# Sample tokens in the MLP's third quarter, a new order for the first up products, and two earlier edits in one kernel

## The chip, the cores and the metric

The kernel runs on one core of a Trainium2 chip. The metric is device time in microseconds (us) of that core for one launch. PE is the matrix engine, DVE the vector engine, ACT the scalar engine, POOL the general engine, SP the engine whose queue starts most transfers. L94 is line 94 of the kernel before.

## The reference, cut to what matters

One layer of an encoder for 1024 prompt frames (one new stream) and 64 sample frames (one running stream with 512 cached frames), 1088 tokens together, D = 1024, in float32. Prompt and sample have their own conditioning vector, so gates, shifts and scales differ between the two.

```python
mod = silu(c) @ w_ada + b_ada                 # shift1, scale1, gate1, shift2, scale2, gate2
h = rms_norm(x, g_norm1) * (1 + scale1) + shift1
proj = h @ w_in                               # parts for attention (MLA) and for gated linear attention (GLA)
a_out = attention(...)                        # low-rank q; latent keys and values; RMS norm of q and k per head
b_out = gla(...)                              # log_a = log_sigmoid(gate_lr @ w_gate_up + b_gate_up) / 16
x = x + gate1 * (concat(a_out, b_out) @ w_out)
h2 = rms_norm(x, g_norm2) * (1 + scale2) + shift2
x = x + gate2 * (square(relu(h2 @ w_up)) @ w_down)
```

Besides x, the new latents, rotary keys and the GLA states are returned.

## The kernel before, in words

**Products.** A float32 product is made of three products in a rounded format: each operand is split into a high part (a cast on ACT, helper line L102 or the line that calls it) and a low part (a subtraction on DVE, L103 or L106). L94, L95 and L96 are the three matmuls. PE's queue is the longest of all.

**Order of the program.** The kernel is written as generators (streams). `interleave` runs them in turns; each `yield pe, wait, cond` says how long PE is taken to work on what was just written, how long the stream then stands back, and what it waits for. A scheduling layer then sets each engine's order by its own costs, so an edit in one place also shifts instructions elsewhere. At run time every engine takes its queue strictly in order.

**Stages.** The first 85 us load x and weights and make q and k of GLA (the stream `shifts` loads the 1024-column rows of w_ada, 'raw', which L177 multiplies). Up to about 260 us GLA runs beside the other projections. It needs the gate weights 'wg' (zeroed on POOL at L615, then filled by a transfer in ACT's queue at L616 and one in SP's at L617), a pair of 'glrT' tiles (POOL, L620 and L621) and 'indi'. All of them stand in the pool 'big', whose room is free only when the first stage's tiles are done; L657 is the first product with wg.

**Keys.** `keys_values` (L960 on) makes keys and values of a tile of 128 tokens: four tiles of cached frames and the sample tile (`past_keys`, about 260 to 330 us), then eight prompt tiles beside attention (355 to 562 us). Two product groups g = 0, 1 give two heads each; ACT sums squares into 'ssk' (L984), POOL makes the reciprocal root of all four heads (L988, L989), DVE multiplies 'kn' (L991) and the rotary part 'krt' (L992) by it, and after `yield 0, 4500` PE transposes them (L998, L1005).

**Out projection and second norm.** Tokens are taken in four chunks of 272 (HW), in the order WORDER = (0, 2, 1, 3); half h = c // 2. Chunks 1 and 3 end in 32 sample tokens each, so their parts list has two entries, and each operation with a conditioning vector is done twice. `main` loads GLA's and attention's outputs ('mx') and the output gate ('mr') of the next chunk, makes its operands 'mh' and 'ml', multiplies by w_out, adds into x (L1456), stores it and adds squares into 'acc' (ACT L1463, DVE L1464). `norm2` makes of that sum a row scale (L1478 to L1489) and then h2 (DVE L1495, ACT L1497). Its last chunk, 3, runs beside the first products of the up projection.

**MLP.** Both projections use seven products of half matrices in place of eight (Strassen's scheme). Up: token operands 'ah' and 'al' number 0 to 6 (`tokens`), weights per block j of 128 columns (`weights`, `put`), products (`up`). The order is written by hand: blocks 0 and 1 do products 0 to 3 for the first half of the columns, then for the second, then 5, 4, 6 block by block; blocks 2 to 15 do 0, 1, 2, 5, 3, 4, 6. The results go to memory ('u_d') and are read back for down, whose sums are scaled and added at L1910 and stored at L1914.

## Time and profile before

| | us |
|---|---|
| three runs, median (lowest to highest) | 1357.65 (1357.14 to 1358.04) |
| the profiled execution's own time | 1358.17 |
| its span | 1356.4 |
| PE busy in the span | 1325.8 (98%) |
| DVE, ACT, POOL busy | 894.9, 655.3, 64.5 |
| granted clock of PE over the span | 0.996 |

The profiled execution's time is 1.8 us over its span, and 0.5 us over the median of the runs. PE's busy time is the time in which at least one matmul is under way; what is left of the span, 30.6 us, is idle time of PE. In the timeline a row ends with the idle time ahead of it and with what ended that: `[1.58 <-DVE kn L991]`. A row with x4 merges four instructions. The granted clock (PEclk) says which share of full speed PE was allowed.

### The profile page before, as it was taken

The page shows a single profiled execution, that of the slowest core. Times are in us where ns is not written, and L with a number is a line of the kernel's source. Part 1 is how long each engine was busy: PE and PEld are TensorE (multiplying, and loading weights), DVE is VectorE, ACT ScalarE, POOL GpSimd, SP SyncE. Part 2 cuts the span into 40 slices and gives each one's busy share as a digit, 9 for nine tenths or more (in the row PEclk, how much of TensorE's full clock was granted, in tenths as well). Part 3 has the DMA queues.
Part 4 walks back from the last instruction along what each step waited for, and adds up shares of the span by engine and source line. Part 5 has one row for each costly group of instructions (what it writes and reads, how often), then busy time and mean ns, then how long its engine had stood idle before and what let it go on. Part 6 is the DMA issues. An engine that isn't in the chain of part 4 may idle for free.

```text
span 1356.4 us, 25887 instructions
## 1 busy us (share of the span) xinstructions
PE 1325.8 (98%) x10052; PEld 1257.9 (93%) x10052; DVE 894.9 (66%) x1926; ACT 655.3 (48%) x1634; POOL 64.5 (5%) x110
## 2 busy tenths in 40 slices
PE   9999999989999999999989999999999999999998
PEld 8899999878867788999989999999999999999998
DVE  4898787465576656677799565665636865874554
ACT  5465545443255656753575445444443333433432
POOL 0110010121111100000000000000000000000000
PEclk9999999999999999999999999999999999999999
DMA  9420123324445320573417443444349845543441
GB/s 343 137 74 1 48 76 90 107 83 126 153 129 171 96 89 16 163 209 111 137 40 232 141 156 128 160 139 138 115 168 341 282 152 192 162 125 92 132 124 34
DMA packets 155110, 183.64 MB, mean 135 GB/s; under 512 B 16063, under 2 KB 106475, under 8 KB 154987
## 3 DMA queue, kind: packets, MB, share of 16 engines
q1 hardware_dynamic: 147530, 176.44, 41.0%
q10 hardware_dynamic: 7456, 5.54, 1.3%
q8 instruction: 79, 1.29, 0.4%
q14 instruction: 45, 0.36, 0.1%
HBM read 130.71 MB, written 51.23 MB: 134 GB/s over the span
## 4 chain that ended last, share of the span: by engine, by line
PE 82%; DVE 7%; DMA 4%; ACT 4%; POOL 2%; issue 1%; SPq 0%; ACTq 0%; DVEq 0%; POOLq 0%
PE mm L94 14%; PE mm L96 13%; PE mm L95 13%; PE g L94 6%; PE g L96 6%; PE g L95 6%; PE tp L94 3%; PE tp L95 3%; PE tp L96 3%; PE mm L1076 3%; PE g L1103 2%; PE mm L177 1%; PE g L881 1%; PE tp L1113 1%; POOL ssk L989 1%
## 5 line engine op out<-in xcount | busy, mean ns | idle before, releaser
L102 ACT CAST opers<-quad 128x512 fp32r<-128x512 f32 x112 | 69.4, 620 | 184.6 <-PE mm L96 145.1
L103 DVE TENSOR_TENSOR opers<-quad,opers 128x512 fp32r<-128x512 f32 x112 | 77.2, 690 | 112.3 <-ACT opers L102 112.3
L96 PE MATMUL mm<-opers 128*128 128x272 f32 x448 | 128.9, 288 | 0.0
L94 PE MATMUL mm<-opers 128*128 128x272 f32 x448 | 128.6, 287 | 0.3 <-DVE e L1910 0.3
L95 PE MATMUL mm<-opers 128*128 128x272 f32 x448 | 128.3, 286 | 0.0
L94 PE MATMUL mm<-ah,wh 128*128 128x272 f32 x424 | 122.5, 290 | 2.0 <-ACT wh L102 1.7
L95 PE MATMUL mm<-al,wh 128*128 128x272 f32 x424 | 121.8, 288 | 0.3 <-DVE al L103 0.3
L96 PE MATMUL mm<-ah,wl 128*128 128x272 f32 x424 | 121.6, 288 | 0.0
L94 PE MATMUL mm<-hh,wh 128*128 128x384 f32 (+2 forms) x264 | 90.6, 344 | 0.7 <-ACT wh L321 0.7
L95 PE MATMUL mm<-hl,wh 128*128 128x384 f32 (+2 forms) x264 | 87.2, 330 | 0.0
L96 PE MATMUL mm<-hh,wl 128*128 128x384 f32 (+2 forms) x264 | 86.9, 330 | 0.0
L94 PEld LDWEIGHTS mm<-opers 128*128 128x128 f32 x448 | 84.6, 189 | 0.5 <-issue 0.5
L96 PEld LDWEIGHTS mm<-opers 128*128 128x128 f32 x448 | 84.3, 188 | 0.0
L95 PEld LDWEIGHTS mm<-opers 128*128 128x128 f32 x448 | 84.1, 188 | 0.0
L94 PEld LDWEIGHTS mm<-ah,wh 128*128 128x128 f32 x424 | 80.0, 189 | 3.1 <-ACT wh L102 2.2
L95 PEld LDWEIGHTS mm<-al,wh 128*128 128x128 f32 x424 | 79.8, 188 | 0.5 <-DVE al L103 0.5
L96 PEld LDWEIGHTS mm<-ah,wl 128*128 128x128 f32 x424 | 79.8, 189 | 0.0
L103 DVE TENSOR_TENSOR opers<-ru,opers 128x544 fp32r<-128x544 f32 x108 | 77.6, 719 | 2.2 <-ACT opers L102 2.0
L102 ACT CAST opers<-ru 128x544 fp32r<-128x544 f32 x108 | 69.4, 643 | 13.1 <-PE mm L96 11.7
L102 ACT CAST wh<-ru 128x512 fp32r<-128x512 f32 x67 | 41.1, 618 | 65.7 <-PE g L95 24.6
L103 DVE TENSOR_TENSOR wl<-ru,wh 128x512 fp32r<-128x512 f32 x67 | 45.9, 689 | 35.5 <-ACT wh L102 35.3
L94 PE MATMUL mm<-wh,hh 128*128 128x264 f32 (+3 forms) x216 | 65.9, 305 | 0.0
(410 smaller groups left out, 4241.5 us busy)
## 6 DMA issues: line engine op xcount, KB each, us to landing
ru<-u_d SPq DMA_DIRECT2D x108, 272.0 KB, 2.9
raw<-in_w_ada SPq DMA_DIRECT2D x40, 512.0 KB, 4.2
ru<-in_w_up SPq DMA_DIRECT2D x32, 512.0 KB, 4.1
quad<-in_w_down SPq DMA_DIRECT2D x16, 1024.0 KB, 7.2
u_d<-st SPq DMA_DIRECT2D x60, 272.0 KB, 2.1
u_d<-sc SPq DMA_DIRECT2D x45, 272.0 KB, 2.2
raw<-in_w_in SPq DMA_DIRECT2D x22, 256.0 KB, 3.8
x<-in_xo_T SPq DMA_DIRECT2D x8, 544.0 KB, 6.1
```

The source lines that it names most:

```text
L94: pin(PE.matmul(out, lhsT=ah, rhs=bh, start=first, stop=False, skip_group_check=more))
L95: pin(PE.matmul(out, lhsT=ah, rhs=bl, start=False, stop=False, skip_group_check=more))
L96: pin(PE.matmul(out, lhsT=al, rhs=bh, start=False, stop=last, skip_group_check=more))
L102: ACT.copy(hi, src)
L103: eng.tensor_tensor(out=lo, in0=src, in1=f32(hi), op=ALU.subtract)
L177: mm = PE.matmul(acc[32 * j:32 * j + 32, 0:256], lhsT=scT[:, k, :], rhs=was[k][:, 256 * j:256 * (j + 1)], start=(k == 0), stop=(k == KT - ...
L881: PE.matmul(sc[:n, a, p], lhsT=d[:, w * p + n * a:w * p + n * a + n], rhs=qv[:, :, p, a], start=True, stop=True)
L989: POOL.tensor_tensor(out=ss[:n, 4:8], in0=ss[:n, 4:8], in1=mhalf[:n], op=ALU.pow)
L1076: PE.matmul(sp[:n, :w], lhsT=x[:, hd, :n], rhs=y[:, hd, :w], start=(j == 0), stop=(j == 4))
L1103: PE.matmul(op[:n, 0:P], lhsT=pt[:kw, k, :n], rhs=kvs[kt // 4].v[:kw, kt % 4, hd], start=(kt == 0), stop=(kt == nkt - 1))
L1113: PE.transpose(tp[:kw, k, :n], pr[k0 // 4][:n, P * k:P * k + kw], ident[:n, :n])
```

## The change

Four edits:

1. GLA's constants wg, glrT and indi move to the pool 'gqkp', which exists from the start. POOL zeroes wg and glrT at the start, and SP starts the three transfers right behind the third chunk of x.
2. In `keys_values` POOL makes the reciprocal root of each pair of heads as soon as the pair's squares are there, and DVE multiplies kn and krt pair by pair. The wait ahead of the transposes becomes a parameter, `ahead`: 7000 for the cached frames and the sample tile, 4500 as before for the prompt's tiles.
3. The 64 sample tokens all stand at the end of chunk 2 (the third quarter, second in WORDER); chunks 0, 1 and 3 hold prompt tokens alone. The waits ahead of the norm's first product grow from 2500 to 4500 in all chunks but the last. Down's sums follow: the first half of the tokens has one span, the second three pieces.
4. Blocks 0 and 1 do products 4, 5, 6 in that order, both blocks in each. `weights` and `tokens` follow that order ("w 4" comes before tokens 5, "w 5" before tokens 6). Block 1's products 5 and 6 go to the bank pair tp instead of g; pool st2 has three buffers.

```diff
+    wg = gqkp.tile([97, 256], F32, name="wg")
+    POOL.memset(wg, 0.0)
+    glrT = [gqkp.tile([97, 320], F32, name=f"glrT{j}") for j in range(2)]
...
+    indi = gqkp.tile([P, 2], F32, name="indi")
...
             load_x(2)
+            SP.dma_start(wg[0:16], I["w_gate_up"])
+            SP.dma_start(wg[96:97], I["b_gate_up"])
+            SP.dma_start(indi, I["gla_ind"])
...
-        wg = big.tile([97, 256], F32, name="wg")
-        POOL.memset(wg, 0.0)
-        ACT.dma_start(wg[0:16], I["w_gate_up"])
-        SP.dma_start(wg[96:97], I["b_gate_up"])
...
-    def keys_values(lh, ll, ki, tab, n, kv, slot):
+    def keys_values(lh, ll, ki, tab, n, kv, slot, ahead=4500):
...
+            POOL.tensor_scalar(out=ss[:n, 4 + 2 * g:6 + 2 * g], in0=ss[:n, 2 * g:2 * g + 2], scalar1=ss[:n, 8:9],
+                               scalar2=192 * EPS, op0=ALU.add, op1=ALU.add)
+            POOL.tensor_tensor(out=ss[:n, 4 + 2 * g:6 + 2 * g], in0=ss[:n, 4 + 2 * g:6 + 2 * g], in1=mhalf[:n, 0:2], op=ALU.pow)
             yield 1300, 0, None
-        POOL.tensor_scalar(out=ss[:n, 4:8], in0=ss[:n, 0:4], scalar1=ss[:n, 8:9], scalar2=192 * EPS, op0=ALU.add, op1=ALU.add)
-        POOL.tensor_tensor(out=ss[:n, 4:8], in0=ss[:n, 4:8], in1=mhalf[:n], op=ALU.pow)
...
+        for g in range(2):
+            DVE.tensor_tensor(out=kn[:n, 2 * g:2 * g + 2], in0=kn[:n, 2 * g:2 * g + 2], in1=rs[g], op=ALU.mult)
...
-        yield 0, 4500, None
+        yield 0, ahead, None
...
     def place(c):
-        h, hs = divmod(c, 2)
-        if hs == 0:
-            return h, HALVES[0], ((0, 512 * h, HW, 0),)
-        return h, HALVES[1], ((0, 512 * h + HW, 512 - HW, 0), (1, SEQ + 32 * h, 32, 512 - HW))
+        t0 = c * HW
+        parts = {2: ((0, t0, HW - DEC, 0), (1, SEQ, DEC, HW - DEC)), 3: ((0, t0 - DEC, HW, 0),)}
+        return c // 2, HALVES[c % 2], parts.get(c, ((0, t0, HW, 0),))
...
-                yield 0, 2500, None
+                yield 0, 2500 if end else 4500, None
...
             for j, x in ((4, 22), (5, 21), (6, 12)):
+                if j > 4:
+                    yield 0, 0, has(f"w {j - 1}")
...
-                if j < 2:
-                    yield from put(j, 5, b11, DVE)
                 sub(t2, b21, t2, DVE)
                 yield from put(j, 4, t2, DVE)
+                done.add(f"w 4 {j}")
                 yield 0, 1500, None
+                if j < 2:
+                    yield from put(j, 5, b11, DVE)
+                    done.add(f"w 5 {j}")
+                    yield 0, 1500, None
...
-                    side[j, h] = g_bank()[:, 0:HT // 2]
+                    side[j, h] = (tp_bank if j == 1 else g_bank)()[:, 0:HT // 2]
...
-            order += [(j, i, h) for j in range(2) for i in (5, 4, 6) for h in range(2)]
+            order += [(j, i, h) for i in (4, 5, 6) for j in range(2) for h in range(2)]
...
-        SPANS = ((0, 0, 512), (1, 512, HT))
+        SPANS = (((0, 0, HT),), ((0, 0, HW - DEC), (1, HW - DEC, HW), (0, HW, HT)))
```

What moves, at three places. PE at the first tile of cached frames, around the transposes of kn; before:

```order
L94 MATMUL mm<-wh,hh 128x320
L95 MATMUL mm<-wl,hh 128x320
L998 MATMUL tp<-ident,kn 128x128 x4
L96 MATMUL mm<-wh,hl 128x320
L1005 MATMUL tp<-ident,krt 128x128 x4
L94 MATMUL mm<-wh,hh 128x320
```

and of the change:

```order
L96 MATMUL mm<-wh,hl 128x320
L1001 MATMUL tp<-ident,kn 128x128 x2
L94 MATMUL mm<-wh,hh 128x320
L1001 MATMUL tp<-ident,kn 128x128 x2
L95 MATMUL mm<-wl,hh 128x320
L96 MATMUL mm<-wh,hl 128x320
L94 MATMUL mm<-wh,hh 128x320
L95 MATMUL mm<-wl,hh 128x320
L96 MATMUL mm<-wh,hl 128x320
L1008 MATMUL tp<-ident,krt 128x128 x4
```

The transposes stand in two pairs, and the rotary part's come five matmuls later. From the tile's last latent product (with a few transposes of a latent among them) to the first transposes of kn stand, over the four tiles of cached frames, 20, 18, 18 and 30 matmuls of the projections before, and 18, 31, 48 and 45 now.

DVE at the end of chunk 0's sum of squares in the out projection ('ml0' is the low part of the third chunk's operand, 'acc' the sum); before:

```order
L1456 SCALAR_TENSOR_TENSOR x12_6700<-mm_6848,modT_98,x12_6700 128x272
L1464 TENSOR_TENSOR acc_6735<-acc_6735,sq_6875 128x272
L103 TENSOR_TENSOR ml0_7174<-mx_6888,mh0_7173 128x1088
L1481 TENSOR_SCALAR st_6927<-tp_6923 128x2
L1481 TENSOR_SCALAR st_6927<-tp_6923 16x1
```

and of the change:

```order
L1457 SCALAR_TENSOR_TENSOR x12_6752<-mm_6903,modT_98,x12_6752 128x272
L103 TENSOR_TENSOR ml0_7234<-mx_6943,mh0_7233 128x1088
L1465 TENSOR_TENSOR acc_6790<-acc_6790,sq_6930 128x272
L1271 TENSOR_TENSOR mx_6944<-mx_6944,mr_6945 128x1088
L1457 SCALAR_TENSOR_TENSOR x21_6753<-mm_6950,modT_98,x21_6753 128x208
L1457 SCALAR_TENSOR_TENSOR x21_6753<-mm_6950,modT_98,x21_6753 128x64
L1482 TENSOR_SCALAR st_6996<-tp_6992 128x2
```

The third chunk's operand now stands ahead of the last addition to the sum, and on ACT its gate's silu stands ahead of the last two squares (before: of the last one). PE's product with the sum (L1478, now L1479) comes 12 matmuls later in its queue.

DVE at the start of the up projection, from the sums of half matrices to the token operands 5 ('al4' to 'al6' are their low parts, 'wl' slots hold weights, 'tw' is the half-made weight of product 4); before:

```order
L1392 TENSOR_TENSOR x21_6701<-x21_6701,x22_6702 128x4x272
L106 TENSOR_TENSOR x12_6700<-x12_6700,x22_6702 128x4x272
L103 TENSOR_TENSOR wl0_7833<-ru_7844,wh0_7832 128x512
L1394 TENSOR_TENSOR x12_6700<-x12_6700,x11_6699 128x4x272
L106 TENSOR_TENSOR tw_7934<-ru_7844,tw_7934 128x512
L103 TENSOR_TENSOR al4_8062<-x22_6702,ah4_7810 128x272 x8
L1686 TENSOR_TENSOR st_7900<-st_7900,g_8138 128x272
L103 TENSOR_TENSOR al5_8096<-x21_6701,ah5_7795 128x272 x8
L103 TENSOR_TENSOR wl1_7835<-tw_7934,wh1_7834 128x512
L103 TENSOR_TENSOR al6_8129<-x12_6700,ah6_7794 128x272 x8
```

and of the change:

```order
L1393 TENSOR_TENSOR x21_6753<-x21_6753,x22_6754 128x4x272
L106 TENSOR_TENSOR x12_6752<-x12_6752,x22_6754 128x4x272
L103 TENSOR_TENSOR wl0_7874<-tw_7975,wh0_7873 128x512
L1395 TENSOR_TENSOR x12_6752<-x12_6752,x11_6751 128x4x272
L1698 TENSOR_TENSOR st_7941<-st_7941,g_8141 128x272
L103 TENSOR_TENSOR al4_8087<-x22_6754,ah4_7851 128x272 x8
L106 TENSOR_TENSOR tw_8022<-ru_7924,tw_8022 128x512
L1698 TENSOR_TENSOR st_7983<-st_7983,g_8175 128x272
L103 TENSOR_TENSOR al5_8122<-x21_6753,ah5_7836 128x272
L103 TENSOR_TENSOR wl1_7876<-tw_8022,wh1_7875 128x512
L103 TENSOR_TENSOR al5_8122<-x21_6753,ah5_7836 128x272 x7
L103 TENSOR_TENSOR wl2_7878<-ru_7885,wh2_7877 128x512
```

Product 4's weight for block 0 now stands ready ahead of its tokens, block 1's comes behind them; before, block 0's came behind the tokens of product 5, and operand 6 ahead of any weight for it. On PE the products stand one behind the other, where before those of several products alternated: 130 matmuls lie between the last chunk's broadcast (L1489, now L1490) and the first of product 4.

More of the change, by code (lines that the diff above doesn't have):

```diff
@@ L252, in layer @@
     h, gqk = {}, []
+    wg = gqkp.tile([97, 256], F32, name="wg")
+    POOL.memset(wg, 0.0)
+    glrT = [gqkp.tile([97, 320], F32, name=f"glrT{j}") for j in range(2)]
+    for t in glrT:
+        POOL.memset(t[0:96], 0.0)
+        POOL.memset(t[96:97], 1.0)
+    indi = gqkp.tile([P, 2], F32, name="indi")
     def w_in_cols(a, b):
@@ L613, in layer @@
         bcum = big.tile([P, 2, TOK], F32, name="bcum")
-        wg = big.tile([97, 256], F32, name="wg")
-        POOL.memset(wg, 0.0)
-        ACT.dma_start(wg[0:16], I["w_gate_up"])
-        SP.dma_start(wg[96:97], I["b_gate_up"])
-        glrT = [big.tile([97, 320], F32, name=f"glrT{j}") for j in range(2)]
-        for t in glrT:
-            POOL.memset(t[0:96], 0.0)
-            POOL.memset(t[96:97], 1.0)
         masks = big.tile([P, 6, 64], I32, name="masks")
         ACT.dma_start(masks, I["gla_masks"][:, 1:7])
-        indi = big.tile([P, 2], F32, name="indi")
-        ACT.dma_start(indi, I["gla_ind"])
         SBk = [big.tile([P, 2, 256], F32, name=f"SB{i}") for i in range(3)]
@@ L985, in keys_values @@
             DVE.tensor_copy(kv.v[:n, slot, 2 * g:2 * g + 2], pg[:, :, P:2 * P])
+            POOL.tensor_scalar(out=ss[:n, 4 + 2 * g:6 + 2 * g], in0=ss[:n, 2 * g:2 * g + 2], scalar1=ss[:n, 8:9],
+                               scalar2=192 * EPS, op0=ALU.add, op1=ALU.add)
+            POOL.tensor_tensor(out=ss[:n, 4 + 2 * g:6 + 2 * g], in0=ss[:n, 4 + 2 * g:6 + 2 * g], in1=mhalf[:n, 0:2], op=ALU.pow)
             yield 1300, 0, None
-        POOL.tensor_scalar(out=ss[:n, 4:8], in0=ss[:n, 0:4], scalar1=ss[:n, 8:9], scalar2=192 * EPS, op0=ALU.add, op1=ALU.add)
-        POOL.tensor_tensor(out=ss[:n, 4:8], in0=ss[:n, 4:8], in1=mhalf[:n], op=ALU.pow)
-        rs = ss[:n, 4:8].rearrange("p (h o) -> p h o", o=1).broadcast_to([n, H, P])
-        DVE.tensor_tensor(out=kn[:n], in0=kn[:n], in1=rs, op=ALU.mult)
-        DVE.tensor_tensor(out=kr[:n], in0=R[:n].rearrange("p t d c -> p t (d c)").broadcast_to([n, H, P]),
-                           in1=rs, op=ALU.mult)
+        rs = [ss[:n, a:a + 2].rearrange("p (h o) -> p h o", o=1).broadcast_to([n, 2, P]) for a in (4, 6)]
+        for g in range(2):
+            DVE.tensor_tensor(out=kn[:n, 2 * g:2 * g + 2], in0=kn[:n, 2 * g:2 * g + 2], in1=rs[g], op=ALU.mult)
+        for g in range(2):
+            DVE.tensor_tensor(out=kr[:n, 2 * g:2 * g + 2], in0=R[:n].rearrange("p t d c -> p t (d c)").broadcast_to([n, 2, P]),
+                              in1=rs[g], op=ALU.mult)
         cs = slice(P * slot, P * slot + n)
-        yield 0, 4500, None
+        yield 0, ahead, None
         tp = heads(tp_bank())
@@ L1158, in past_keys @@
             yield 220, 1000, None
-            yield from keys_values(lh, ll, 8 + t, t, P, kvS[0], t)
+            yield from keys_values(lh, ll, 8 + t, t, P, kvS[0], t, 7000)
         yield from new_keys(8)
@@ L1169, in new_keys @@
         if i == 8:
-            yield from keys_values(lh, ll, 12, 4, n, kvN[0], 0)
+            yield from keys_values(lh, ll, 12, 4, n, kvN[0], 0, 7000)
         else:
@@ L1545, in layer @@
         wq = uctx.enter_context(tc.tile_pool(reuse_waits="tile", name="wq", bufs=1))
-        st2_ = pool("st2", 2)
+        st2_ = pool("st2", 3)
         warr = {}
@@ L1626, in rest @@
                 yield 0, 1500, None
+                sub(t2, b21, t2, DVE)
+                yield from put(j, 4, t2, DVE)
+                done.add(f"w 4 {j}")
+                yield 0, 1500, None
                 if j < 2:
                     yield from put(j, 5, b11, DVE)
-                sub(t2, b21, t2, DVE)
-                yield from put(j, 4, t2, DVE)
-                yield 0, 1500, None
+                    done.add(f"w 5 {j}")
+                    yield 0, 1500, None
                 yield from put(j, 6, b22, DVE)
@@ L1643, in weights @@
                     step = next(r)
+            for i in (4, 5):
+                yield 0, 0, has(f"tokens {i} 1")
+                for j, r in ((0, a), (1, b)):
+                    while f"w {i} {j}" not in done:
+                        yield next(r)
+                done.add(f"w {i}")
             yield 0, 0, has("tokens 6 1")
@@ L1717, in product @@
                         relu2("22", 6, True)
-                if i == 4 and h:
+                if i == (5 if j < 2 else 4) and h:
                     a11, a21, a22 = acc.pop((j, "11")), acc.pop((j, "21")), acc.pop((j, "22"))
@@ L1906, in out @@
             e = OUT[c][:, m]
-            for s, c0, c1 in SPANS:
+            for s, c0, c1 in SPANS[th]:
                 c0, c1 = max(c0, h * HW), min(c1, h * HW + HW)
@@ L1936, in _tables @@
     return {"k_rope_tab": np.ascontiguousarray(tab), "gla_masks": masks, "gla_ind": ind}
-ORDER = np.r_[0:512, SEQ:SEQ + 32, 512:SEQ, SEQ + 32:TOK]
+ORDER = np.r_[0:752, SEQ:TOK, 752:SEQ]
 _OUTS = [("y_T", (D, TOK), None),
```

1 line of the change is left out of this document (removed).

## The prediction

> **What bounds the kernel now.** I read first how busy each engine is in each stage (a table by stretches of the span; the first three columns are length, PE's busy time with its count of instructions, and weight loads, then DVE, ACT, POOL; the last three are granted clock, DMA share, GB/s).
>
> ```profile
> core 0: us, PE busy (x) PEld busy (x) DVE busy (x) ACT busy (x) POOL busy (x), PEclk, DMA share, GB/s
> 0.00:85.00 85.00, 81.56 (x643) 73.59 (x644) 60.45 (x146) 43.86 (x86) 4.79 (x12) 1.00 0.61 204
> 85.00:260.00 175.00, 170.83 (x1221) 160.76 (x1220) 131.54 (x305) 93.09 (x324) 16.86 (x30) 1.00 0.22 64
> 260.00:330.00 70.00, 63.81 (x393) 56.82 (x392) 42.92 (x107) 33.64 (x130) 14.28 (x26) 1.00 0.33 94
> 355.00:562.00 207.00, 199.19 (x1402) 160.62 (x1402) 139.80 (x406) 125.76 (x397) 23.58 (x34) 0.99 0.38 117
> 562.00:681.00 119.00, 117.19 (x918) 115.99 (x917) 82.19 (x180) 59.66 (x125) 4.75 (x8) 0.99 0.52 154
> 681.00:716.00 35.00, 31.52 (x221) 29.61 (x222) 33.28 (x80) 24.57 (x65) 0.24 (x1) 0.95 0.22 65
> 716.00:1353.00 637.00, 636.68 (x5098) 636.27 (x5096) 396.89 (x689) 271.60 (x507) 0.00 (x0) 1.00 0.49 158
> ```
>
> PE sets the time everywhere. The number of matmuls hardly changes (7 rows more of 8542 in PE's order), so a gain can only be PE's idle time, length minus busy: 3.4, 4.2, 6.2, 7.8, 1.8, 3.5 and 0.3 us in these stages. The last 637 us have nothing to give. A second loss hides inside busy time: where the granted clock is below 1, PE works slower. Two-microsecond stretches show it (columns: length, PE busy, clock, DMA share, GB/s):
>
> ```profile
> 596.00:598.00 2.00, 2.00 (x16) 0.88 1.09 372
> 598.00:600.00 2.00, 2.00 (x11) 0.50 1.11 279
> 600.00:602.00 2.00, 2.00 (x13) 0.77 0.63 208
> 404.00:406.00 2.00, 2.00 (x10) 0.50 0.50 129
> 704.00:706.00 2.00, 1.76 (x8) 0.50 0.36 139
> ```
>
> Around 598 the clock is halved for 0.48 + 2.00 + 0.92 = 3.4 us (twice the missing share of each row) and PE loses 2 x (0.12 + 0.50 + 0.23) = 1.7 us. The same happens around 404 and 704. The two of 598 and 704 come right behind waits which this change works on.
>
> **The change part by part: GLA's constants.** PE waits at the first gate product; the second row is the transfer's issue, the third its size and microseconds to landing:
>
> ```profile
> 91.51 1.10 PE L657 MATMUL g<-glrT,wg 97*128 97x256 f32 x4 [1.06 <-POOL SB L629]
> 87.97 0.43 ACTq L616 DMA_DIRECT2D wg<-in_w_gate_up  x1
> wg<-in_w_gate_up ACTq DMA_DIRECT2D x1, 16.0 KB, 3.4
> 43.32 0.64 PE L177 MATMUL mm<-raw,scT 128*32 128x256 f32 x8 [1.19 <-DMA raw<-in_w_ada]
> ```
>
> The first row names POOL, but 87.97 + 3.4 = 91.4 is when PE starts: it is the transfer. With the issue at the start of the kernel, 1.06 us go. In PE's new order 18 matmuls instead of 14 stand ahead of the fourth group of L177: four more, at 81.56 / 643 = 0.13, take 0.5 of its wait of 1.19. The three added issues stand in SP's queue ahead of the loads of w_ada; at 0.43 each they would cost 1.3 if SP had no time there, and this wait would grow by as much. The stage's DMA share of 0.61 leaves room, so I take no delay and keep 1.3 as the end. Together -1.6 (+0.2 to -2.3).
>
> **Keys.** Waits for the multiplied keys at L998 (total, times, longest; first those of 255 to 330 us, then those of 355 to 562 with another wait of that stage), and the chain ahead of the first:
>
> ```profile
> PE tp L998 <- DVE kn L991: 4.0, 3, 1.6
> ```
>
> ```profile
> PE tp L1113 <- ACT prob L1087: 3.5, 3, 1.2
> PE tp L998 <- DVE kn L991: 1.7, 2, 0.9
> ```
>
> ```profile
> 271.14 0.31 POOL L988 TENSOR_SCALAR ssk<-ssk 128x4 f32<-128x4 f32 x1 [3.70 <-ACT krt L984]
> 271.53 1.03 POOL L989 TENSOR_TENSOR ssk<-ssk,mhalf 128x4 f32<-128x4 f32 x1
> 272.60 0.69 DVE L991 TENSOR_TENSOR kn<-kn,ssk 128x512 f32<-128x512 f32 x1 [1.11 <-POOL ssk L989]
> 273.44 0.63 PE L998 MATMUL tp<-ident,kn 128*128 128x128 f32 x4 [1.58 <-DVE kn L991]
> 266.88 0.55 POOL L122 TENSOR_TENSOR s<-s,mhalf 128x1 f32<-128x1 f32 x1
> 268.01 0.42 DVE L700 TENSOR_TENSOR lat<-cn,gkv_bc 128x256 f32<-128x256 f32 x1
> ```
>
> From the last square to kn the work was 0.31 + 1.03 + 0.69 = 2.03. The power of one column took 0.55 and of four 1.03, so two are about 0.71 (0.55 + 0.48 / 3); half of kn is 0.42. The chain of the second pair becomes 0.31 + 0.71 + 0.42 = 1.44, 0.6 shorter. At the first tile two fewer matmuls stand ahead, at 63.81 / 393 = 0.16 that is 0.3 lost, but two transposes and a matmul (0.3 + 0.16) now cover the second pair: 1.58 - 0.6 + 0.3 - 0.45, about 0.8, is left. The next two tiles have 13 and 30 more matmuls ahead, 2.1 and 4.8 us, more than any of these waits. So 4.0 becomes 0.8: -3.2. For the prompt's tiles `ahead` is unchanged; the shorter chain takes 0.6 of each of two waits: -1.2 (0 to -1.7). DVE pays 2 x 0.42 - 0.69 = 0.15 twice on each of 13 tiles, 3.9 us, and POOL as often a second start; DVE's 139.80 busy of 207 and 42.92 of 70 hide it. If DVE were the late one there, all of this gain would turn round (rival A).
>
> **The sum of chunk 0 in the out projection.** PE waits 1.78 for it, and DVE had waited for ACT's last square:
>
> ```profile
> 595.75 0.71 PE L1478 MATMUL tp<-ones,acc 128*128 128x1 f32 x6 [1.78 <-DVE acc L1464]
> 595.16 0.44 DVE L1464 TENSOR_TENSOR acc<-acc,sq 128x272 f32<-128x272 f32 x1 [2.57 <-ACT sq L1463]
> 593.70 1.11 ACT L1267 ACTIVATE mr<-mr 128x1088 f32<-128x1088 f32 x1 [1.99 <-DMA mr<-r_d]
> 595.03 1.08 ACT L102 CAST mh<-mx 128x1088 fp32r<-128x1088 f32 x1
> 596.15 1.29 DVE L103 TENSOR_TENSOR ml<-mx,mh 128x1088 fp32r<-128x1088 f32 x1 [0.54 <-ACT mh L102]
> 588.34 1.20 SPq L1418 DMA_DIRECT2D mr<-r_d  x2
> 587.03 1.28 DVE L1268 TENSOR_TENSOR mx<-mx,mr 128x1088 f32<-128x1088 f32 x1
> ```
>
> The last square stood behind a silu that waited for a transfer, whose buffer came free when L1268 ended (587.03 + 1.28, the issue at 588.34). Two things now pull against each other. PE's product comes 12 matmuls later, 12 x 117.19 / 918 = 1.5 us. But cast and subtraction of the next operand stand ahead of the last square's addition: with the silu still at 593.70 the sum would be done at about 593.70 + 1.11 + 0.4 + 1.08 + 1.29 + 0.44 = 598.0, 2.4 later than before (595.16 + 0.44), and the wait would grow by 0.9. In DVE's new order, however, the gate's multiplication stands ahead of a subtraction (1.29) and an addition, so the transfer starts some 1.7 earlier and so does the silu: the sum comes 0.7 later, PE 1.5 later, and 1.0 of the wait goes (bounds +0.9 and -1.78). A remaining 0.8 is below the waits followed by a half clock; I take that stretch of 1.7 us as gone.
>
> The chunk with the samples now comes second, with three SP issues and twice the DVE additions more. The stage's idle time of 1.8 is the 1.78 of this one wait, so no other operand was late. I put that at nothing; uncovered it is the three issues, at most 3 x 0.6 = 1.8.
>
> **The start of up.** DVE prepares the last chunk and the operands, PE waits at the products:
>
> ```profile
> 681.47 0.93 PE L1489 MATMUL tp<-last,ones 128*128 128x128 f32 x6
> 682.43 3.13 DVE L1495 SCALAR_TENSOR_TENSOR x<-x,G,tp 128x240 f32<-128x240 f32 x11
> 687.48 1.31 DVE L1495 SCALAR_TENSOR_TENSOR x<-x,G,tp 128x32 f32<-128x32 f32 x5
> 698.20 0.68 DVE L106 TENSOR_TENSOR tw<-ru,tw 128x512 f32<-128x512 f32 x1
> 698.80 2.90 DVE L103 TENSOR_TENSOR al<-x,ah 128x272 fp32r<-128x272 f32 x8
> 700.27 0.39 PE L94 MATMUL mm<-ah,wh 128*128 128x272 f32 x1 [1.30 <-ACT wh L102]
> 702.11 0.39 PE L94 MATMUL g<-ah,wh 128*128 128x272 f32 x1 [1.01 <-DVE st L1686]
> ```
>
> Before, the low half of operand 4 began to come at 698.80 + 0.36 (2.90 / 8) = 699.2. Now 8 operations of 272 columns replace 16 (4.44 together; 8 x 0.4 = 3.2, so -1.2), the half-made weight (-0.68) moves behind, one addition of a result, 0.4, comes ahead: 697.7 by the old clock. PE has 130 x 0.128 = 16.6 us of matmuls after 681.47 + 0.93 and reaches product 4 at 699.0. The operand is there, by a margin of 1.3. Block 1's weight follows at 697.7 + 2.5 + 0.68 and a cast, about 701.5; PE needs it after 48 matmuls, at 705.1. Of the stage's 3.5 us of idle time I leave 0.4, less than one operation, for some late operand: -3.1. With the waits the half clock at 704 goes: -1.7.
>
> [...]
>
> **Sum.** -1.6 - 3.2 - 1.2 - 1.0 - 1.7 - 3.1 - 1.7 = -13.5. Against it: in three stages (85 to 260, 260 to 330, 355 to 562) the scheduling layer has shifted many instructions, and waits like those of L1113 for ACT's 'prob' in attention (3.5 in three, above) can arise or go. I allow one such wait, 3.5 / 3 = 1.2, per stage: +3.5 (0 to +7). Net -10.0. The profiled execution took 1358.17 (span 1356.4 and 1.8 around it), 0.5 over the median, so 1348.2 by the profile and **1347.7** as a median.
>
> **The rivals.** 0.2% is 2.7 us, about what a measurement of this kernel tells from no change; the bounds are 1354.9 and 1360.4.
>
> A: in the first 560 us waits only change place. DVE and ACT carry the same chains, and a later transpose lets the next group's operand be late. For it: attention has 7.8 of idle time spread over several causes; against it, DVE is at 68% there. Then the first two parts' 6.0 are lost, with no allowance beside it: -7.5, 1350.2.
>
> B: the half clock stays. For it: the wait of 1.58 at 273.44 lies in a stage whose clock reads 1.00, so a wait alone doesn't decide. Against it: all three stretches follow waits. Net -10.0 + 3.4 = -6.6: 1351.1.
>
> C, slower: in the attention stage the pairs of transposes stand in PE's order ahead of their operands, tile after tile, because each pair now passes through POOL and DVE. At the 1.58 seen for the first cached tile, for eight prompt tiles, that is 12.6, and with a half clock behind every second one (4 x 1.7 = 6.8) 19.4 against -10.0: 1367.1. It decides from (10.0 + 2.7) / 8 = 1.6 us a tile. Against it: two waits in eight tiles before, at most 0.9.
>
> D, the change does not do what it says: each removed wait of PE returns at the next operand, because transfers and DVE set the pace; about 1357.
>
> **How the numbers follow.** The main case 0.52, A 0.15, B 0.15, D 0.08, C 0.10. Main, A and B are faster by more than 0.2%: 0.82; same 0.08; slower 0.10. The main case reaches from 1342 (all allowance unused, the remaining waits gone too) to 1351.2 (3.5 more); A and B with the same 3.5 to 1354.5. The range 1342.0 to 1354.5 leaves out C and D.
>
> **What would show it.** Right: no wait at L657; PE's idle time in 260 to 330 near 3 us in place of 6.2; the product with chunk 0's sum waiting under 1 us and the clock at 1.00 behind it; less than 1 us idle at the start of up, again at full clock. Each stage's idle time, set beside the table above, tests one term. Wrong: idle time in attention above 7.8 (A or C), a half clock without a wait ahead of it (B), or operand 2 of the out projection late. If span and idle time part ways, the clock or the length of single matmuls has changed, and my account by idle time fails.

## The result and the profile after

| | before | changed |
|---|---|---|
| median of four runs, us | 1357.39 | 1344.83 |
| lowest to highest | 1355.59 to 1358.04 | 1344.16 to 1345.33 |
| profiled execution, span | 1356.4 | 1343.2 |
| PE busy, idle in the span | 1325.8, 30.6 | 1320.6, 22.6 |
| granted clock over the span | 0.996 | 0.999 |

The ratio is 0.9908, with a 95% interval of 0.989 to 0.9925: 12.6 us faster, where about 10 were forecast. Two executions below ran at a low mean clock (0.654 for one of the kernel before, 0.866 for one of the kernel called f2, which is the profiled one); they are left out of all figures, and f2's kernel was run again, as g3, for its trace.

The stages of the changed kernel, in the same columns as before:

```profile
core 0: us, PE busy (x) PEld busy (x) DVE busy (x) ACT busy (x) POOL busy (x), PEclk, DMA share, GB/s
0.00:85.00 85.00, 81.45 (x635) 72.36 (x636) 59.33 (x144) 43.41 (x85) 6.39 (x17) 1.00 0.62 205
85.00:260.00 175.00, 171.82 (x1233) 162.23 (x1232) 133.13 (x308) 93.96 (x326) 15.15 (x25) 1.00 0.22 64
260.00:330.00 70.00, 65.56 (x404) 60.01 (x403) 43.41 (x116) 33.29 (x128) 18.48 (x36) 1.00 0.39 111
355.00:562.00 207.00, 201.09 (x1444) 163.88 (x1444) 142.81 (x424) 130.71 (x402) 29.78 (x50) 1.00 0.38 114
562.00:681.00 119.00, 117.36 (x915) 116.25 (x915) 85.05 (x182) 58.90 (x128) 6.01 (x8) 0.99 0.50 151
681.00:716.00 35.00, 34.99 (x278) 34.71 (x276) 34.02 (x72) 23.09 (x54) 0.00 (x0) 1.00 0.50 164
```

Length minus busy gives PE's idle time: 3.6, 3.2, 4.4, 5.9, 1.6 and 0.0 us, against 3.4, 4.2, 6.2, 7.8, 1.8 and 3.5. (The stages now begin up to 13 us earlier, so a border cuts a little elsewhere; between fixed instructions the start of up, from the last chunk's sum to the first product of down, has 0.3 against 3.5.) Hardly anything is gained at the sum of chunk 0, all of the wait at the start of up is gone, and the keys' stages lie between. The clock column answers the second half of the question. The half-clocked stretches of before at 403 and 703 are absent, the one behind the sum is there as before (columns: length, PE busy, clock, DMA share, GB/s):

```profile
590.00:592.00 2.00, 1.10 (x9) 1.00 1.00 341
592.00:594.00 2.00, 2.00 (x12) 0.52 0.90 218
594.00:596.00 2.00, 2.00 (x12) 0.62 0.95 286
596.00:598.00 2.00, 2.00 (x16) 1.00 1.04 354
```

It loses 2 x (0.48 + 0.38) = 1.7 us, as each of the three did. So the span's 13.2 us are 8.0 of idle time, 3.4 of two stretches, and 1.8 inside PE's busy time that I did not take apart. Part of the last may be the price of starting again: behind this wait the first product took 0.23 to the next start, from 591.53 to 591.76, where the second took 0.13:

```profile
591.53 0.39 PE L94 MATMUL mm<-mh,wh 128*128 128x272 f32 x1
591.76 0.29 PE L95 MATMUL mm<-ml,wh 128*128 128x272 f32 x1
591.89 0.28 PE L96 MATMUL mm<-mh,wl 128*128 128x272 f32 x1
```

**Cached frames and samples.** These are the waits of PE between 255 and 330 us:

```profile
PE tp L1008 <- ACT cl L713: 1.3, 1, 1.3
PE tp L1001 <- DVE kn L993: 1.2, 1, 1.2
PE tp L710 <- DVE cn L696: 0.8, 1, 0.8
PE tp L710 <- ACT mog L830: 0.6, 1, 0.6
PE tp L1153 <- DVE kr L1010: 0.4, 1, 0.4
PE tp L1153 <- DVE kl L1003: 0.2, 1, 0.2
```

The waits for kn shrank from 4.0 to 1.2, but 1.3 appeared at the transposes of krt (L1008), which now wait for ACT to have made a latent output 'cl' from a tp bank, and 0.6 at the transposes of the next cached latents (L1153). The chain of the first cached tile, pair by pair:

```profile
269.03 0.46 POOL L986 TENSOR_SCALAR ssk<-ssk 128x2 f32<-128x2 f32 x1 [2.22 <-ACT krt L984]
269.58 0.71 POOL L988 TENSOR_TENSOR ssk<-ssk,mhalf 128x2 f32<-128x2 f32 x1
270.76 0.54 POOL L986 TENSOR_SCALAR ssk<-ssk 128x2 f32<-128x2 f32 x1 [0.48 <-ACT krt L984]
271.38 0.71 POOL L988 TENSOR_TENSOR ssk<-ssk,mhalf 128x2 f32<-128x2 f32 x1
```

```profile
272.12 0.42 DVE L993 TENSOR_TENSOR kn<-kn,ssk 128x256 f32<-128x256 f32 x1 [0.57 <-POOL ssk L988]
```

```profile
270.89 0.41 PE L1001 MATMUL tp<-ident,kn 128*128 128x128 f32 x2
272.60 0.44 PE L1001 MATMUL tp<-ident,kn 128*128 128x128 f32 x2 [1.15 <-DVE kn L993]
```

The first pair is transposed 1.7 us before the second, and only the second waits, 1.15. The power of two columns took 0.71, as interpolated; the addition ahead of it took 0.54, not the 0.31 carried over.

**The sum of chunk 0.** One engine's row after the other (SP's issue, ACT, DVE, PE):

```profile
580.80 0.52 SPq L1419 DMA_DIRECT2D mr<-r_d  x1
582.37 0.37 SPq L1420 DMA_DIRECT2D mx<-mix_d  x1
```

```profile
585.29 1.11 ACT L1270 ACTIVATE mr<-mr 128x1088 f32<-128x1088 f32 x1 [3.08 <-DMA mr<-r_d]
587.97 1.11 ACT L102 CAST mh<-mx 128x1088 fp32r<-128x1088 f32 x1 [1.25 <-DMA mx<-mix_d]
588.98 0.42 ACT L1464 ACTIVATE sq<-x 128x272 f32<-128x272 f32 x1
```

```profile
589.11 1.29 DVE L103 TENSOR_TENSOR ml<-mx,mh 128x1088 fp32r<-128x1088 f32 x1 [1.50 <-ACT mh L102]
590.31 0.43 DVE L1465 TENSOR_TENSOR acc<-acc,sq 128x272 f32<-128x272 f32 x1
```

```profile
590.89 0.71 PE L1479 MATMUL tp<-ones,acc 128*128 128x1 f32 x6 [1.64 <-DVE acc L1465]
```

The silu did come earlier, 585.29 here against 593.70, more than the general shift of 5 to 6. But the cast behind it waited for the attention half of the next operand, whose transfer started after the gate's and landed at 587.97. The last square and the last addition stood behind that cast and its subtraction, so that PE waited 1.64 in spite of its 12 matmuls more.

### The profile page after: what moved, and what is told of

Same layout as the page of the kernel before. It is cut to its first block, busy times and chain, and to the rows that moved or that the text cites. A ratio compares the mean times of both kernels' runs of the same rounds, so it can differ in the third digit from the quotient of the medians.

```text
span 1343.2 us, 25901 instructions
## 1 busy us (share of the span) xinstructions
PE 1320.6 (98%) x10052; PEld 1255.2 (93%) x10052; DVE 891.1 (66%) x1920; ACT 653.5 (49%) x1626; POOL 75.9 (6%) x136
## 4 chain that ended last, share of the span: by engine, by line
PE 83%; DVE 7%; DMA 3%; ACT 3%; issue 1%; POOL 1%; SPq 0%; ACTq 0%; DVEq 0%; POOLq 0%
PE mm L94 15%; PE mm L96 14%; PE mm L95 14%; PE g L94 6%; PE g L96 6%; PE g L95 5%; PE mm L1079 3%; PE tp L94 3%; PE tp L96 3%; PE tp L95 3%; PE g L1106 2%; PE g L881 2%; PE tp L1116 1%; PE mm L177 1%; PE mm L130 1%
## 5 line engine op out<-in xcount | busy, mean ns | idle before, releaser
L102 ACT CAST opers<-ru 128x544 fp32r<-128x544 f32 x108 | 69.4, 643 | 13.2 <-PE mm L96 10.9
```

Source lines behind the costliest of these rows:

```text
L102: ACT.copy(hi, src)
```

## The experiments

All times below are medians beside runs of the kernel before on the same chip. Runs of one program scatter by several us, and most of that is the clock: of 34 runs of before beside the first four kernels, those with a mean granted clock of 0.999 averaged 1355.2, of 0.997 1357.1, of 0.996 1357.8 and of 0.993 1362.2 (4, 10, 11 and 3 runs). One stretch of half clock is 1.7 of 1356 us, 0.0013 of the clock. I therefore give the mean clock, and a time at full clock: each run's time less its span times the missing clock, averaged (before: 1352.9 in the first two groups, 1353.0 in the third). Since the clock is listed to 0.001, one such run is uncertain by 0.7 us.

### Each edit alone

e1 has the rows of the diff for wg, glrT and indi, and nothing else of it:

```diff
+    wg = gqkp.tile([97, 256], F32, name="wg")
...
+            SP.dma_start(wg[0:16], I["w_gate_up"])
```

> The kernel before with the first edit alone: GLA's constants loaded at the start. Theory (each edit takes away its own waits, so the four add up to the 12.6 us): the wait of 1.06 at the first gate product goes and 0 to 0.5 of that for w_ada, -1.0 to -2.0 us. Rival (the edits work only together, what one frees is waited for elsewhere): within 0.5 us of before, with the 1.06 found again at a later product.

e2 has `keys_values` in pairs with `ahead` = 7000 for cached frames and samples:

```diff
+            POOL.tensor_tensor(out=ss[:n, 4 + 2 * g:6 + 2 * g], in0=ss[:n, 4 + 2 * g:6 + 2 * g], in1=mhalf[:n, 0:2], op=ALU.pow)
...
+        yield 0, ahead, None
```

> The kernel before with the second edit alone: keys scaled in pairs of heads, and the longer wait ahead of the transposes for cached frames and samples. Theory (own waits only): idle time between the first gate product and the start of the out projection falls by 3 to 5 us, and so does the time; if the half clock inside attention goes with it, 1.7 more. Rival (waits change place): -1 us or less, with the waits for prob, v or qrl longer than before.

e3 has the new places of the samples and the norm's wait:

```diff
+        parts = {2: ((0, t0, HW - DEC, 0), (1, SEQ, DEC, HW - DEC)), 3: ((0, t0 - DEC, HW, 0),)}
...
+                yield 0, 2500 if end else 4500, None
```

> The kernel before with the third edit alone: samples in the third quarter, longer wait ahead of the norm. Theory (own waits only): the sum of chunk 0 still makes PE wait about 1.6 with a half clock behind it, as in the changed kernel; eight operations instead of sixteen on DVE take 1 to 2 us off the idle time at the start of up: -1 to -2. Rival (third and fourth edit need each other): no gain, within 0.5 us, because the waits at the start of up are for weights and for operand order, not for the last chunk.

e4 has the order of the products of blocks 0 and 1, with weights and tokens following it, the other banks and the third buffer of st2:

```diff
+            order += [(j, i, h) for i in (4, 5, 6) for j in range(2) for h in range(2)]
```

> The kernel before with the fourth edit alone: products 4, 5, 6 in order, both blocks together. Theory (own waits only): the idle 3.5 us at the start of up falls to about 1 and the half clock there goes, -3.5 to -5. Rival (third and fourth edit need each other): the last chunk's sixteen operations leave operand 4 late by about 1.2 - 1.3 + 0.9, one wait of some 1 us with a half clock behind it stays, -1.5 or less.

Measured, the kernel before at 1357.62 beside them, and the changed kernel from a later run (c, below) beside its own before:

| kernel | median (runs) | ratio, 95% interval | mean clock | at full clock | idle in its profile |
|---|---|---|---|---|---|
| e1 | 1359.13 (12) | 1.0006, 0.9989 to 1.0023 | 0.9962 | 1353.5 | 28.9 |
| e2 | 1355.62 (12) | 0.9986, 0.9971 to 1.0001 | 0.9971 | 1351.1 | 28.6 |
| e3 | 1354.76 (12) | 0.9979, 0.9967 to 0.9992 | 0.9964 | 1350.1 | 28.7 |
| e4 | 1354.32 (12) | 0.9973, 0.9957 to 0.999 | 0.9967 | 1350.4 | 27.9 |
| changed (c) | 1346.07 (5) | 0.9898, 0.9881 to 0.9915 | 0.9992 | 1344.6 | 22.5 |

In sum the idle times add up: 1.7 + 2.0 + 1.9 + 2.7 = 8.3 less than the 30.6 of before, and all four together have 8.1 less. Stage by stage the agreement is partly chance. This is PE's idle time in each profile, between fixed instructions:

| | start to first gate product | to the out projection | to the first product of down |
|---|---|---|---|
| before | 4.69 | 16.92 | 5.29 |
| e1 | 3.20 | 16.80 | 5.23 |
| e2 | 4.70 | 14.30 | 5.85 |
| e3 | 3.31 | 16.68 | 5.18 |
| e4 | 4.47 | 16.59 | 3.15 |
| changed, first profile | 3.85 | 13.22 | 1.96 |
| changed, c | 2.83 | 14.07 | 2.09 |

Each edit's own stage is the first column for e1, the second for e2, the third for e3 and e4. There they take away 1.5, 2.6, 0.1 and 2.1, in all 6.4, and all four together 7.9. Of e3's 1.9, 1.4 lie in the first column, which it does not touch. So the first, second and fourth edit take away waits of their own, while the third does so hardly by itself: with the fourth it is worth about 1 us more than the two alone, and the rival by which these two need each other holds in part. (Each row is one profile; the two of the changed kernel differ by up to 1.0 in a column.)

e1's profile has no wait for the transfer at L657 any more, and yet its runs are not faster: -1.0 to -2.0 was expected, and 0.8 more came out, with an interval from -1.5 to +3.1 us. e2 idles 2.6 us less between the first gate product and the out projection, a little under the 3 to 5 expected, and 1.2 more at the start of up; its time fell by 2.0, with an interval that just includes no change. e3 gained 2.9 where 1 to 2 were expected, but not as expected: its sum waits 2.3 us, not 1.6, and the start of up lost 0.6, not 1 to 2. Its waits do not account for its gain. e4 gained 3.3, just under the 3.5 to 5 expected. At the start of up, e4 left 1.5 of 3.5 us and e3 2.9, and neither has a half clock there in its profile. This is e4, waits between 670 and 720 us:

```profile
PE g L94 <- DVE st L1697: 0.6, 1, 0.6
PE mm L95 <- DVE al L103: 0.3, 1, 0.3
PE mm L94 <- ACT wh L102: 0.2, 1, 0.2
PE mm L96 <- DVE wl L103: 0.2, 1, 0.2
```

The weight's wait of 1.30 has become 0.2 without the third edit. What is left are waits on DVE, which still has the last chunk's sixteen operations to do; with the eight of the third edit, in the changed kernel, they are gone.

The loss to the clock does not add up. The four kernels lose 5.2, 3.9, 4.9 and 4.5 us to it (span times missing clock), before 5.1 beside them, the changed kernel 1.1. Where the stretches stand in the profiles tells part of it. The one near 403 follows this wait of the kernel before, in attention:

```profile
401.75 0.46 PE L1113 MATMUL tp<-ident,prob 64*128 64x64 f32 x4 [1.07 <-ACT prob L1087]
```

e1, e3 and e4 have the same wait (1.05 to 1.07) and a stretch behind it. The eight profiles of kernels with keys in pairs (among them e2 and those below) have neither: in seven no wait of PE for 'prob' is left there, in f1 one of 0.4. The stretch at the start of up is in before, e1 and e2, and in no profile with the third or the fourth edit. The one behind the sum stays in e1, e3 and e4, in e3, where the wait is longer (2.3), for 6.8 us; in e2, where it is 1.2, it is absent.

### The changed kernel in many runs

> The changed kernel itself, in many runs beside the kernel before on one chip. Two parts of the 12.6 us are asked for: idle time of PE (8.0 less in the profiles) and half-clocked stretches (each 1.7 us; the kernel before has a mean clock of 0.9963 over 35 runs, so nearly three). Theory 1 (the waits bring the half clock on, so that fewer waits mean fewer stretches): mean clock 0.9985 or more over all runs, and 11 to 13 us below before. Theory 2 (the stretches come as they like, the runs so far were lucky): mean clock 0.996 to 0.997, and 7 to 9 us below before.

Measured: 1346.07 against 1359.51, 13.4 less, at a mean clock of 0.9992; the five clocks lie between 0.998 and 1.0, those of before at 0.9955 on average beside it. The numbers are those of theory 1: the better clock belongs to the kernel and was not luck. That waits bring the half clock on, this run alone does not show; the runs further below ask for it. At full clock the difference is 1352.9 - 1344.6 = 8.3, about the idle time (8.1); the other 5 us are missing clock (6.2 us of it in the runs of before beside it, 1.1 in the changed kernel).

### Which half of the keys' edit works

f1 takes the longer wait back, here and in the same way for the sample tile; f2 takes the pairs back:

```diff
-            yield from keys_values(lh, ll, 8 + t, t, P, kvS[0], t, 7000)
+            yield from keys_values(lh, ll, 8 + t, t, P, kvS[0], t)
```

> The changed kernel with the wait ahead of the transposes back at 4500 for cached frames and samples; the scaling in pairs stays. Theory (the later place in PE's queue is what takes away the waits of the cached frames' tiles): 1 to 3 us of waits for kn come back between 270 and 330 us, time +1 to +3. Rival (the shorter chain does it): within 0.5 us, kn waits below 1.5 in all there.

Measured: 1346.27 beside the changed kernel's 1346.07 (ratio to before 0.9902, 0.9886 to 0.9919), clock 0.9988. The rival holds for the time: beside the pairs, the later place in PE's queue is worth nothing. Its own waits for kn between 255 and 330 us are larger than the rival said:

```profile
PE tp L1001 <- DVE kn L993: 3.0, 5, 1.0
PE tp L710 <- ACT mog L830: 0.6, 1, 0.6
PE tp L710 <- DVE cn L696: 0.5, 1, 0.5
```

But they are five short ones in place of three long ones of before, and in the changed kernel the place of the 1.8 that the later transposes save is taken by the bank's 1.3 and smaller waits. From the first gate product to the first transposes of 'prob', which holds the cached frames' tiles, f1 idles 8.5 us, the changed kernel 8.4 and 9.0 in its two profiles, before 9.8.

f2 and its repetition g3, cut to the scale's rows (those of POOL, kn and krt go back with them):

```diff
-        rs = [ss[:n, a:a + 2].rearrange("p (h o) -> p h o", o=1).broadcast_to([n, 2, P]) for a in (4, 6)]
+        rs = ss[:n, 4:8].rearrange("p (h o) -> p h o", o=1).broadcast_to([n, H, P])
...
```

> The changed kernel with the scaling of all four heads at once as before; the wait of 7000 ahead of the transposes stays. Theory (the later place does it for cached frames, the pairs only for prompt tiles): 0.5 to 1 us more at the first cached tile and 0.5 to 1.5 more in attention, time +1 to +2.5. Rival (pairs are worth nothing, they only add work on POOL and DVE): -0.5 to +0.5.

> The kernel with all four heads scaled at once and the wait of 7000 (the earlier run's profile was a disturbed one), for its trace. Its undisturbed times were 1348.5 to 1354.2 at clocks of 0.995 to 0.997. Theory (one long wait for kn per tile in place of two short ones puts more than about 2 us of missing work in single windows): kn waits over 1.3 us at L991 and two or more stretches of half clock before 560 us. Rival (the idle time itself is larger): idle time 3 us or more above the changed kernel's 22.5 with at most one stretch.

Measured: 1350.35 over five runs of f2 and 1350.43 over four of g3 (ratios 0.9936, 0.9916 to 0.9956, and 0.9936, 0.9921 to 0.9951), clocks 0.9964 and 0.9975. That is some 4 to 5 us slower than the changed kernel, more than any of my numbers; at full clock it is 1.4 and 2.0 (1346.0 and 1346.6), so most of the difference is clock. g3's profile has 25.9 us of idle time, 3.4 more than c, at full clock; its waits between 255 and 556 us:

```profile
PE tp L998 <- DVE kn L991: 3.0, 3, 1.3
PE tp L1113 <- ACT prob L1087: 2.3, 2, 1.2
PE tp L1005 <- ACT cl L713: 1.6, 1, 1.6
PE tp L710 <- DVE cn L696: 1.4, 1, 1.4
PE tp L1057 <- ACT mt L1219: 1.1, 1, 1.1
```

So the rival's idle time is what this profile shows, and of the theory's two stretches it shows none; the three runs beside it had clocks of 0.996 and 0.997, but where in them the clock was missing is not known.

Where the idle time lies settles which half works where. Up to the first transposes of 'prob' g3 idles 8.8 us, no more than the changed kernel: at the cached frames' tiles the later transposes alone (g3) do as well as the pairs alone (f1), and both together no better. From there to the out projection g3 idles 7.5, before 7.2, the changed kernel 4.8 and 5.1, f1 4.6. So it is at the prompt's tiles, beside attention, that the pairs are worth 2.4 us or more. There PE waits for kn 1.6 in two waits (0.4 in c) and for 'prob' 3.5 in three (2.5), and the wait of before at 401 is back:

```profile
398.54 0.46 PE L1113 MATMUL tp<-ident,prob 64*128 64x64 f32 x4 [1.06 <-ACT prob L1087]
```

### What brings the half clock on

f3 puts the product with the sum 30 matmuls later, in all chunks but the last, g2 in chunk 0 alone:

```diff
-                yield 0, 2500 if end else 4500, None
+                yield 0, 2500 if end else 8500, None
```

```diff
-                yield 0, 2500 if end else 4500, None
+                yield 0, 2500 if end else 8500 if c == WORDER[0] else 4500, None
```

> The changed kernel with the wait ahead of the norm's first product at 8500 in place of 4500 (not in the last chunk): PE's product with the sum comes 30 matmuls, 3.8 us, later, more than the 1.64 us which it waits now. Theory 1 (half clock follows the wait): no wait at the sum, the half-clocked stretch behind it gone, -1.6 in idle time and -1.7 in clock, in all -2.5 to -3.5. Theory 2 (half clock independent of the wait): -1.2 to -1.8, a stretch still there or elsewhere. Rival to both: the later norm makes up's first operands late, 0 or slower.

> The changed kernel with the product of the sum put 30 matmuls later for chunk 0 alone, the other chunks as in the changed kernel. Theory (the later norm of the chunks 2 and 1 was what brought 1.3 us of waits to the start of up in the run with all of them later): no wait at the sum, full clock, idle time at the start of up 0.3 to 0.5 again; 1342 to 1343.5. Rival (chunk 0's norm itself is what the operands of up wait for): waits of 1 us or more at the start of up remain, 1344.5 to 1346.

Measured: f3 1345.42 (ratio 0.9904, 0.9885 to 0.9923), g2 1344.12 (0.989, 0.9875 to 0.9905); clocks 0.9997 and 0.9998, the highest of all. Both profiles have no wait at the sum and no stretch behind it, as theory 1 said. But 2.5 to 3.5 us were not gained, because the wait came back one step on: in f3 at the start of up, in g2 at the product that spreads the norm's scale.

```profile
PE g L94 <- DVE st L1698: 1.1, 2, 0.9
```

```profile
593.57 0.64 PE L1479 MATMUL tp<-ones,acc 128*128 128x1 f32 x6
598.99 1.00 PE L1490 MATMUL tp<-dg,ones 128*128 128x128 f32 x6 [1.57 <-DVE dg L1486]
```

Of g2's theory the idle time is as it said (0.2 at the start of up), and neither its time nor the rival's was met. g2 has the lowest median of all kernels tried, but its interval and that of the changed kernel overlap by most of their width, so it is not shown to be faster.

g1 fills the wait at the sum instead, with six products whose result nothing uses:

```diff
+                for _ in range(6 if c == WORDER[0] else 0):
+                    PE.matmul(pm[:, 0:P], lhsT=ones, rhs=ident, start=True, stop=True)
```

> The changed kernel with six extra matmuls (128x128, their result is overwritten and used by nothing) ahead of the product with chunk 0's sum: they fill 1.4 to 1.6 us of the 1.64 us in which PE waits there, so work is added and the end of the wait does not move. Theory 1 (a stretch of half clock comes behind a window of 3.4 us in which PE lacks work for about 2 us): the stretch behind the sum goes, mean clock 0.9995 or more, -0.5 to -1.7 us against the changed kernel's 1345 to 1346. Theory 2 (the stretch has to do with something else at that place, the transfers for example): a stretch at the same place, no gain.

Its PE at that place, and its clock there:

```profile
589.62 1.50 PE L1479 MATMUL tp<-ident,ones 128*128 128x128 f32 x12
592.09 0.74 PE L1481 MATMUL tp<-ones,acc 128*128 128x1 f32 x6 [0.97 <-DVE acc L1465]
```

```profile
592.00:594.00 2.00, 1.91 (x16) 1.00 1.01 320
594.00:596.00 2.00, 2.00 (x17) 1.00 0.58 90
```

The stretch is gone, at the same place and under the same load of transfers (a DMA share of 1.01; 1.00 and 0.90 in the changed kernel's rows from 590 to 594). In time the kernel got slower, 1348.33 (0.9928, 0.9915 to 0.994): the sum came later than 590.74, the scale's product then waited another 1.0, and 2.2 us of idle time returned at the start of up, perhaps since the extra products had shifted the order of the rest. As a test of the time it failed. Of the clock it is one profile, with a mean clock of 0.9994 over five runs, hardly apart from the 0.9992 without the fill, and by the estimate explained next, the piece ahead of the place still lacks 1.9 us of work, hardly less than the 2.0 in c, where the stretch came. So it does not decide between the two theories; f3 and g2, without the wait, speak for the first.

The traces of the thirteen profiles say more. In their records of the granted clock each stretch that the end of the span does not cut off is one or two pieces of 3.413 us (three of one piece in the profile before, one in the changed one, 6.8 us in e3 and g4), and each begins a whole number of such pieces after the first full clock (in the profile before 395.95 us = 116 pieces, in the changed one 587.09 = 172). I cut each trace into these pieces and added up, for each, the time in which PE did not start matmuls at their usual distance: idle time, the slower start behind it, and the one-column products of a sum. These are estimates from the start times of PE's matmuls in the traces. Of the pieces at full clock that miss 2.2 us or more, nine, every one is followed by half clock, while of those that miss less than 1.9 none is. Between 1.9 and 2.2 both happen, six with half clock behind them and fourteen without; seven of the fourteen are at products with 32 of 128 columns in use (L177), which the estimate counts badly, and one at the very end. So in these profiles, by this estimate, a stretch came behind a piece that was short of work for some 2 or more of its 3.41 us. A single wait does not tell it: behind the one of 1.64 at the sum in the changed kernel a stretch came, behind the one of 1.58 at 273.44 in the kernel before none did (the clock of that stage reads 1.00); what else falls into the same piece may decide.

By the same estimate, how a wait lies to the border of two pieces may count too. The first full clock came 4.8 to 7.1 us after the span's start in the thirteen profiles (7.02 before, 5.00 in the changed one), so pieces counted from there fall on other places of the program in each. g3 waits longer at the sum than the changed kernel, 2.08 against 1.64, and no stretch follows:

```profile
593.53 0.71 PE L1476 MATMUL tp<-ones,acc 128*128 128x1 f32 x6 [2.08 <-DVE acc L1462]
```

Its first full clock was at 5.53, so by this count a border would stand 172 pieces later, at 592.62, in the middle of this wait (591.45 to 593.53). Its wait of 1.06 for 'prob' would be cut in the same way, by a border at 398.06, while in the profile before the same wait (400.68 to 401.75) lies whole between 399.55 and 402.96, where the stretch begins. Part of the scatter between runs of one kernel may come from this; no run here sets the border at will, so it is not shown to be the cause.

### Without the first edit

g4 is the changed kernel with GLA's constants back in their old place:

```diff
-    wg = gqkp.tile([97, 256], F32, name="wg")
...
+        wg = big.tile([97, 256], F32, name="wg")
...
```

> The changed kernel without its first edit, GLA's constants loaded where they were. Theory (the wait of 1.06 and part of that for w_ada were real): +1.0 to +2.0 us against the changed kernel's 1345 to 1346, idle time before the first gate product 0.8 to 1.5 larger. Rival (the time gained there is waited away later, as the first edit alone gained nothing): within 0.5 us, with idle time up to 260 us the same.

Measured: 1347.21 (0.9915, 0.9901 to 0.9928), 1.1 above the changed kernel's median on the same chip and 1.9 above that of all its nine runs (1345.33), with overlapping intervals. At full clock it is 1344.4, no slower; its profile waits 2.5 at the sum and has a stretch of 6.8 us behind it, so that its clock has another cause than the constants. Its first gate product waits as predicted and now names the transfer itself:

```profile
PE g L657 <- DMA wg<-in_w_gate_up: 0.8, 1, 0.8
```

In the eight profiles with the early constants (the changed kernel's two among them) the idle time up to the first gate product averages 3.0 us, in the five without 4.2 (2.6 to 3.9 against 3.3 to 4.7). The wait is real, and about 1.2 us are gone; that this shortens the whole is not shown, neither by e1 nor by g4.

## Why the prediction was right, and by how much not

The range held the time, and the main case's mechanism, fewer and shorter waits of PE and fewer stretches of half clock, is what the profiles show. That the parts came to nearly the forecast sum is in part luck: several terms were too large, and others which were in no term made up for them. By its own steps:

**Constants, -1.6.** The transfer was the true releaser (g4 names it), the 1.06 are gone. The wait for w_ada scatters: 1.19 before and 1.3 in the changed kernel's profile, but 0.3 in c. Over the eight profiles with the early constants it averages 0.5, over the five without 0.9, so most of this step's half microsecond is seen on average, and no delay by the added issues. What is left of the 1.6 cannot be told in the time.

**Keys of cached frames, -3.2.** The idle time of the stage fell by 1.8. The step that failed is the overlap, "13 and 30 more matmuls ahead, more than any of these waits": the later transposes did remove waits, but a bank in use then made them wait, which I had only as part of the allowance. The pairs alone (f1) and the later place alone (g3) leave the same idle time as both.

**Keys of the prompt, -1.2.** The waits for kn fell by 0.4 only (1.7 to 1.3, of which 0.9 is a new one at the first prompt tile), while the whole stage lost 1.9 of idle time. So the size came out by causes that I had not priced: 1.2 less for 'prob' (3.5 to 2.3), 0.6 less for the output 'mt', and behind them the half clock.

**The sum of chunk 0, -1.0, and its half clock, -1.7.** This failed: 1.64 of 1.78 us are still waited and the stretch is there. By the step's own numbers (0.7 later for the sum, 1.5 for PE) 0.8 should have gone and 1.0 remained, not the other way round. The step "the transfer starts some 1.7 earlier and so does the silu" was right and not enough; the cast that now stands ahead of the last square waits for another transfer, which I had taken as landed.

**Start of up, -3.1, and its half clock, -1.7.** Right: 0.3 us are left of 3.5, at full clock. No wait is left at product 4, and e4 alone (1.5 left, e3 alone 2.9) shows the order of the weights to be the larger part.

**Allowance, +3.5.** It stood for three stages. In 85 to 260 us nothing arose beside the wait for the constants: the 1.0 lost there is that wait. In 260 to 330 new waits of 1.9 came, partly in place of others, and the stage fell 1.4 short of its term; in attention 0.7 more went than its term. So some 0.7 of the 3.5 was used.

**The shortfall.** The forecast's net of 10.0 was 6.6 of idle time and 3.4 of clock; the span lost 8.0, 3.4 and the 1.8 of busy time that no term held. The clock's 3.4 came from another place: the stretch at the sum, counted as gone, is still there, and the one at 403, in no term, is gone with the wait for 'prob' ahead of it. That these two are of one size is luck.

**The rivals.** A fell: the three stages from 85 to 562 us have 4.6 us less idle time. B, the half clock staying, fell as a whole: the mean clock rose from 0.9955 to 0.9992 beside it; at the sum, where the wait stayed (1.78 before, 1.64 now), the stretch stayed too. C and D fell with the sign.

What stays open: the loss to the clock hardly fell with any single edit (by 1.1 us at most) and by 4 to 5 with all of them. The stretches near 403 and at the start of up go with their waits in the profiles, but the runs' mean clocks do not add up from that; that pieces short of work in different places add up in one is possible, but no run here shows it. What makes up the 1.8 us of busy time, and e3's gain, is open as well.

## What to carry to other kernels

Where PE sets the time, count its idle time by stage and, beside it, the pieces of half clock: in this kernel between a quarter and two fifths of the gain was clock (3.4 of 13.2 us in the profiles, 5.1 of 13.4 over the runs). Breaking one chain into two shorter ones (the pairs of heads) paid twice here: 2.4 us or more of idle time beside attention, and most of the 4 to 5 us without it was clock. Moving a waiting instruction back in its queue gained little here where something behind it came late: at the transposes (1.3 at L1008), at the sum (still 1.64) and at the norm (1.57 in g2) a wait stayed or reappeared one step on. And an edit's idle time belongs to it only in the stage that it touches: of the third edit's 1.9 us, 1.4 lay elsewhere.

## What the runs showed of the hardware

The scatter between runs of one program was mostly the clock: 1355.2 us on average at a mean clock of 0.999 and 1362.2 at 0.993, for the kernel before on the same chip. The half clock came in pieces of 3.413 us, and in these profiles behind pieces that by my estimate from the traces lacked 1.9 to 2.8 us of work. Behind the wait of the changed kernel at 591 us the first product of 272 columns took 0.23 us to the next start, those in the stream ahead of it (from 588.34) 0.12 to 0.13. On POOL the addition to two columns of 'ssk' took 0.37 us on average (24 of them in the changed kernel's profile; the two shown, 0.46 and 0.54, are slow ones) where that to four took 0.33 (12 before), so that two of the halves took more than twice the whole. The power took 0.70 for two columns and 1.03 for four there, but 1.04 for the two columns of the norm's scale in the same profile, so the number of columns alone does not set it.
